# Two sets of tiles that swap parts between the projections and the FFN, the FFN's norm issued behind the projections, and LoRA's second stages among r, k and v

## The chip, the cores and the metric

The kernel runs on one core of one Trainium2 chip. The metric is the time of the whole program on the device in microseconds (us); lower is better. Six streams of instructions run side by side on the core: TensorE (PE, with its weight loads shown as PEld), VectorE (DVE), ScalarE (ACT), GpSimd (POOL), SyncE (SP), which only issues DMAs here, and the DMA engines.

## The reference, cut to what matters

Two layers over 1024 tokens of width 1024, one batch. Each layer is a mixer and an FFN, each behind an RMSNorm that is scaled and shifted by a condition `c`:

```python
for l in range(DEPTH):                                   # DEPTH = 2
    sh1, sc1, gt1, sh2, sc2, gt2 = jnp.split(cond @ ada_w[l] + ada_b[l], 6)
    h = _rmsnorm(x, norm1_g[l]) * (1 + sc1) + sh1
    rw_r, rw_k, rw_v, gl_q, ..., rt_g = jnp.split(h @ w_in[l], splits)   # 24 tiles of 128 columns
    y_a = _rwkv7_mixer(h, rw_r, rw_k, rw_v, ...)   # r, k, v mixed with the token before; w, a, g (and
                                                   # v's residual in layer 1) through LoRA: (f(xw @ w1)) @ w2
    y_b = _gla_mixer(h, ...); y_c = _retention_mixer(...)
    x = x + gt1 * (concat(y_a, y_b, y_c) @ w_out[l])
    h = _rmsnorm(x, norm2_g[l]) * (1 + sc2) + sh2
    x = x + gt2 * ((silu(h @ w_gate[l]) * (h @ w_up[l])) @ w_down[l])    # 2816 wide: 22 tiles
return _rmsnorm(x, norm_f_g)
```

## The kernel before, in words

Activations lie with features on the 128 partitions and 512 tokens (one half, `hf` 0 or 1) along a row. Every large product is done by `dense` (L198): for each of eight (or, in the FFN's last product, three or four) tiles of the contraction it issues three matmuls of 128x128 weights by 512 columns: weight's high part by activation's high part (L207), high by low (L208), low by high (L209). All three add into one PSUM bank of the pool `psd`, which has two. The weight's high part `wh` is a cast by ACT (L186), its low part `wl` a subtraction on POOL (L187); both have three buffers, so the cast for a later tile waits until an earlier product has read its `wh`.

An activation that feeds `dense` is a pair of such parts. In the kernel before, the normed `h` is 8 pairs of 514 columns in the pool `hp`, of which `dense` reads 512 from the third on; the one column before them is the last token of the first half, so that a read shifted by one column is the token shift. The gated products of the FFN and the mixers' output `y` are pairs `gh`, `gl` of 512 columns in the pool `ffn`, read from the first column on.

The order of the work is written out by hand. Main line, (l, hf) for layer and half: `project(0,0)`, `project(0,1)`, then for each half `w_out` (mixers' output through `w_out`, residual), a norm, `ffn`; between the halves' FFNs stands the next layer's `project`. So: `ffn(0,0)`, `w_out(0,1)`, `project(1,0)`, `ffn(0,1)`, `w_out(1,0)`, `project(1,1)`, `ffn(1,0)` with `w_out(1,1)` ahead of its last product, `ffn(1,1)`. The mixers run behind this line as generators in `streams`: after each three matmuls `dense` calls `pump(0.65)`, which lets a stream issue steps worth 0.65 times its rate. `heads` is GLA and retention, `mixers` the RWKV recurrence (a triangular solve of 31 steps on DVE, L914 and L916, per unit of 128 tokens). `drain` runs what is left of the streams at once. A scheduler in the framework then settles the order on each engine.

`project` issues the heads' 13 products (`heads_tiles`), starts the stream of heads (`early`), does LoRA's first stages (`lora_ab`, or `lora_first` in the first call), and then `rkv(p)` for four tiles of 128 columns: three products, each evacuated by ACT (L534), then DVE (L535), and in the first half by a one-column copy on ACT (L538). `lora2(p)` makes LoRA's second stages of tile p: w and a (two matmuls each), in layer 1 u (one), and o (one in f32), L555. w, a and u are evacuated by a tanh on ACT (L404), after which DVE (L405) works in SBUF; o is evacuated by a copy on DVE (L560). In `project(0,0)` `lora2(p)` follows `rkv(p)`. In the other three all four stand after all of `rkv` (`LQ = 3`).

The two `layer_start` calls, around `project(1,0)` and `project(1,1)`, also make the normed `h` for the FFN that follows. Its square sums run as a stream from the start, but its eight steps (`norm`) are passed to `project` as `side`, of which `lora2` takes one after each of its groups: `hp` has room for one `h` alone, and the projections read it to the end. Then `drain` issues the rest of `heads`, and `mixers` starts with the FFN.

Of the kernel before, what the change touches and what calls it, by code (L numbers as in the profile page):

```python
# [10 lines left out]
F32 = mybir.dt.float32  # L11
# [24 lines left out]
LQ = 3  # L36
# [31 lines left out]
XPB = 11  # L68
AHEAD = 60
# [25 lines left out]
def trunk_kernel(ctx, tc, xT, cT, ada_w, pv, wfm, wo, wg, wu, wd, l1w, l2a, l2g, l2c,  # L95
# [163 lines left out]
    def rstd_of(x, idle=None):  # L259
# [29 lines left out]

    def norm_h(x, l, hf, which, h, pool=hp, r=None, mods=None, E=V, idle=None):  # L290
# [36 lines left out]
    def hact(h, shift=0):  # L327
        return lambda k, part: h[k][part][:, 2 - shift:514 - shift]
# [25 lines left out]
    def project(l, hf, h, pool, ip, early=None, first=None, side=None):  # L354
# [173 lines left out]
        def rkv(p):  # L528

            for j in range(3):  # L530
# [11 lines left out]
                more()  # L542

        def lora2(p):
            pcol = slice(p * 128, (p + 1) * 128)
            a = slice(512 + p * 128, 512 + (p + 1) * 128)
            for name, pairs, b_ in (("w", ((l2s[:, pcol], lw), (l2l[0:64, pcol], lw[0:64])), "w0"),
                                    ("a", ((l2s[:, a], la), (l2l[64:128, pcol], la[64:128])), "a0"),
                                    ("u", ((l2v[:, pcol], lv[0:96]),) if l else None, "v0"),
                                    ("o", ((l2gs[:, pcol], lg),), None)):  # L550
                if pairs is None:
                    continue
                ps = bank()
                for i, (w_, a_) in enumerate(pairs):
                    T.matmul(ps, w_, a_, start=i == 0, stop=i == len(pairs) - 1)  # L555
                t = ev()
                if b_:
                    sigmoid(t, ps, l, b_, p)
                else:
                    V.tensor_copy(t, ps)  # L560
                keep(ip, name, t, p)
                step(side)
            if p == 3:
                ip["units"] = True

        if first:
# [496 lines left out]
    def pair_tiles(pool):  # L1063
        return [pool.tile([128, 512], F32R, tag=t, name=t, bufs=8) for t in ("gh", "gl")]

    def y_load(l, hf, y, pool):
        for k in KO:
# [3 lines left out]
            split(t, y[k][0], y[k][1])  # L1071
# [17 lines left out]
    def ffn(l, hf, x, h, before_last=None, side=None):  # L1089
# [6 lines left out]
        def gate_up(f, gt):  # L1096
# [7 lines left out]
            gt.append(pair_tiles(gp))  # L1104
            split(sg, *gt[-1])
# [267 lines left out]
```

## Time and profile before

| | |
|---|---|
| time, median of 3 runs (lowest to highest) | 3398.83 us (3397.83 to 3406.38) |
| time of the profiled execution | 3401.25 us |
| its span | 3399.5 us |
| TensorE clock granted, mean share of full | 0.92 |
| busy: PE / DVE / ACT / POOL | 3049.9 / 1994.5 / 1113.9 / 1234.7 us |
| three matmuls on `h` (L207 to L209) | 2208 of each, 423, 411 and 410 ns |
| three matmuls on `gh`, `gl` | 960 of each, 419, 401 and 400 ns |

Busy time of PE overlaps itself: a matmul is counted from its start to its modelled end, and the next one starts before that. So the spacing of starts, not the mean duration, tells the rate. The clock is either full (1.00) or half (0.50); a stretch's figure is the mean.

### The profile page before, as it was taken

The page shows a single profiled execution, that of the slowest core. Times are in us where ns is not written, and L with a number is a line of the kernel's source. Part 1 is how long each engine was busy: PE and PEld are TensorE (multiplying, and loading weights), DVE is VectorE, ACT ScalarE, POOL GpSimd, SP SyncE. Part 2 cuts the span into 40 slices and gives each one's busy share as a digit, 9 for nine tenths or more (in the row PEclk, how much of TensorE's full clock was granted, in tenths as well). Part 3 has the DMA queues.
Part 4 walks back from the last instruction along what each step waited for, and adds up shares of the span by engine and source line. Part 5 has one row for each costly group of instructions (what it writes and reads, how often), then busy time and mean ns, then how long its engine had stood idle before and what let it go on. Part 6 is the DMA issues. An engine that isn't in the chain of part 4 may idle for free. (4 is left out here: it accounts for less than half of the span.)

```text
span 3399.5 us, 47488 instructions
## 1 busy us (share of the span) xinstructions
PE 3049.9 (90%) x18162; PEld 2326.1 (68%) x18162; DVE 1994.5 (59%) x3747; ACT 1113.9 (33%) x1703; POOL 1234.7 (36%) x825
## 2 busy tenths in 40 slices
PE   6897888799888888999988999899997989999998
PEld 4664666476676676776766777677576767778886
DVE  6565777576776655536766663624666666452223
ACT  4324323243233223524322322542432322342222
POOL 6313333123334334532333434533232433444443
PEclk8988889799989898999988999999897989999999
DMA  6744535434544224434433322543533323332332
GB/s 230 239 157 142 169 110 156 153 103 128 147 129 113 88 84 133 156 90 146 129 98 86 87 70 87 161 130 112 155 83 88 105 80 94 120 109 87 105 92 82
DMA packets 266835, 411.01 MB, mean 121 GB/s; under 512 B 71152, under 2 KB 149424, under 8 KB 266608
## 3 DMA queue, kind: packets, MB, share of 16 engines
q1 hardware_dynamic: 211312, 393.28, 37.2%
q10 hardware_dynamic: 55296, 14.70, 2.1%
q8 instruction: 143, 2.34, 0.3%
q14 instruction: 84, 0.69, 0.1%
HBM read 343.92 MB, written 63.96 MB: 120 GB/s over the span
## 5 line engine op out<-in xcount | busy, mean ns | idle before, releaser
L187 POOL TENSOR_TENSOR wl<-wr,wh 128x1024 fp32r<-128x1024 f32 (+2 forms) x508 | 1028.6, 2027 | 1744.2 <-ACT wh L186 1653.2
L207 PE MATMUL psd<-h,wh 128*128 128x512 f32 (+1 forms) x2208 | 933.2, 423 | 112.7 <-DVE sg L1100 65.7
L208 PE MATMUL psd<-h,wh 128*128 128x512 f32 (+1 forms) x2208 | 908.1, 411 | 12.1 <-DVE h L195 12.0
L209 PE MATMUL psd<-h,wl 128*128 128x512 f32 (+1 forms) x2208 | 905.1, 410 | 0.0
L186 ACT CAST wh<-wr 128x1024 fp32r<-128x1024 f32 (+2 forms) x507 | 440.8, 871 | 1142.0 <-PE psd L208 582.2
L207 PEld LDWEIGHTS psd<-h,wh 128*128 128x128 f32 (+1 forms) x2208 | 432.1, 196 | 249.9 <-DVE sg L1100 74.3
L208 PEld LDWEIGHTS psd<-h,wh 128*128 128x128 f32 (+1 forms) x2208 | 434.7, 197 | 117.2 <-DVE h L195 15.8
L209 PEld LDWEIGHTS psd<-h,wl 128*128 128x128 f32 (+1 forms) x2208 | 433.7, 196 | 103.2 <-issue 2.4
L207 PE MATMUL psd<-gh,wh 128*128 128x512 f32 x960 | 401.0, 419 | 25.9 <-DVE x L1114 14.0
L208 PE MATMUL psd<-gl,wh 128*128 128x512 f32 x960 | 385.0, 401 | 6.1 <-DVE gl L195 6.1
L209 PE MATMUL psd<-gh,wl 128*128 128x512 f32 x960 | 384.0, 400 | 0.0
L207 PEld LDWEIGHTS psd<-gh,wh 128*128 128x128 f32 x960 | 184.7, 193 | 78.6 <-issue 24.1
L1114 DVE SCALAR_TENSOR_TENSOR x<-psd,mod,x 128x512 f32<-128x512 f32 x192 | 143.2, 748 | 130.0 <-PE psd L209 128.4
L208 PEld LDWEIGHTS psd<-gl,wh 128*128 128x128 f32 x960 | 185.6, 193 | 47.0 <-DVE gl L195 9.3
L209 PEld LDWEIGHTS psd<-gh,wl 128*128 128x128 f32 x960 | 185.4, 193 | 40.6 <-POOL wl L187 0.3
L914 DVE TENSOR_TENSOR tm<-X,nl 128x60 f32<-128x60 f32 (+24 forms) x496 | 189.0, 381 | 14.6 <-DMA nl<-nd 0.2
L242 DVE SCALAR_TENSOR_TENSOR aw<-aw,cb 128x1024 f32<-128x1024 f32 x96 | 128.4, 1341 | 100.0 <-DMA aw<-in_ada_w 75.8
L916 DVE TENSOR_TENSOR X<-X,tm 128x60 f32<-128x60 f32 (+24 forms) x496 | 165.1, 333 | 15.3
L1100 DVE SCALAR_TENSOR_TENSOR sg<-sg,psd 128x512 f32<-128x512 f32 x88 | 60.1, 683 | 194.1 <-ACT sg L1099 193.9
L1103 DVE SCALAR_TENSOR_TENSOR sg<-sg,psd 128x512 f32<-128x512 f32 x88 | 60.1, 683 | 141.0 <-PE psd L209 140.8
L195 DVE TENSOR_TENSOR gl<-sg,gh 128x512 fp32r<-128x512 f32 x88 | 96.3, 1094 | 37.0 <-ACT gh L194 36.9
L277 DVE TENSOR_TENSOR acc<-acc,sq 128x512 f32<-128x512 f32 x63 | 96.3, 1528 | 30.9 <-ACT sq L270 29.4
(459 smaller groups left out, 3526.6 us busy)
## 6 DMA issues: line engine op xcount, KB each, us to landing
aw<-in_ada_w SPq DMA_DIRECT2D x96, 512.0 KB, 3.9
wr<-in_wfm SPq DMA_DIRECT2D x96, 512.0 KB, 3.7
wr<-in_wg SPq DMA_DIRECT2D x88, 512.0 KB, 3.6
wr<-in_wu SPq DMA_DIRECT2D x88, 512.0 KB, 3.6
wr<-in_wd SPq DMA_DIRECT2D x128, 256.0 KB, 2.7
wr<-in_wo SPq DMA_DIRECT2D x32, 512.0 KB, 3.6
wr<-in_wd SPq DMA_DIRECT2D x64, 192.0 KB, 2.4
x<-in_xT SPq DMA_DIRECT2D x32, 256.0 KB, 4.5
```

The source lines that it names most:

```text
L186: (E.copy if E is A else E.tensor_copy)(wh[:, :n], wr[:, :n])
L187: WS.tensor_tensor(out=wl[:, :n], in0=wr[:, :n], in1=f32(wh[:, :n]), op=ALU.subtract)
L195: E.tensor_tensor(out=lo, in0=src, in1=f32(hi), op=ALU.subtract)
L207: T.matmul(ps[:M], sh, act(k, 0), start=(k == order[0]), stop=False)
L208: T.matmul(ps[:M], sh, act(k, 1), start=False, stop=False)
L209: mark[:] = [T.matmul(ps[:M], sl, act(k, 0), start=False, stop=(k == order[-1])).ins]
L242: V.scalar_tensor_tensor(out=w, in0=w, scalar=0.5, in1=cb, op0=ALU.mult, op1=ALU.mult, accum_out=mod[l][:, rnd, k:k + 1])
L277: V.tensor_tensor(out=acc, in0=acc, in1=sq, op=ALU.add)
L914: V.tensor_tensor(out=tm[:, :nr, :n], in0=X[:, :nr, s:s + 1].to_broadcast([128, nr, n]), in1=nl[:, s, s + 1:32].unsqueeze(1).to_broadcast( ...
L916: V.tensor_tensor(out=X[:, :nr, s + 1:32], in0=X[:, :nr, s + 1:32], in1=tm[:, :nr, :n], op=ALU.add)
L1100: V.scalar_tensor_tensor(out=sg, in0=sg, scalar=1.0, in1=pg, op0=ALU.add, op1=ALU.mult)
L1114: V.scalar_tensor_tensor(out=x[m], in0=ps, scalar=mod[l][:, 5, m:m + 1], in1=x[m], op0=ALU.mult, op1=ALU.add)
```

## The change

- `h`, gated products and `y` use one kind of tile, `pair_tiles`: a row of 528 columns (`HP = 16` and 512), of which `dense` reads from column 16 on.
- There are two sets of 16 such tiles, `sa` in `hp` and `sb` in `ffn`. The set that holds a projection's `h` takes the gated products of the FFN behind it; the other holds that FFN's `h`. Then they swap.
- So the FFN's norm no longer waits for the projections' last read. In `layer_start` it becomes a stream of its own at rate 0.8, started with the projections; what is left of it at their end is issued there.
- `lora2` makes one name of one tile. `rkv` spreads these among its 12 products: one after each (12 in layer 0), or one, one, two (16 in layer 1).
- In `layer_start` the streams are no longer drained: `later` runs `heads`, and goes on to `mixers` once the projection is over.
- The squares at the very start have four buffers instead of five.

```diff
+HP = 16
@@ rstd_of
-                sq = idle.tile([128, 512], F32, tag="sq", name="sq", bufs=5)
+                sq = idle.tile([128, 512], F32, tag="sq", name="sq", bufs=4)
+    def pair_tiles(pool):
+        return [pool.tile([128, HP + 512], F32R, tag="h", name="h", bufs=16) for _ in range(2)]
@@ norm_h
-            h.append([pool.tile([128, 514], F32R, tag="h", name="h", bufs=16) for _ in range(2)])
+            h.append(pair_tiles(pool))
-            hi, lo = (h[k][j][:, 2:514] for j in range(2))
+            hi, lo = (h[k][j][:, HP:] for j in range(2))
     def hact(h, shift=0):
-        return lambda k, part: h[k][part][:, 2 - shift:514 - shift]
+        return lambda k, part: h[k][part][:, HP - shift:HP + 512 - shift]
@@ project
-        def rkv(p):
-            for j in range(3):
+        def rkv():
+            todo2 = [(p, n) for p in range(4) for n in ("waoh" if not l else "wauo") if n != "h"]
+            n2 = len(todo2)
+            for t3 in range(12):
+                p, j = divmod(t3, 3)
                 i = 4 * j + p
                 ps = dense(get_w(wfm[l, i]), act)
...
                 more()
+                while n2 - len(todo2) < (t3 + 1) * n2 // 12:
+                    lora2(*todo2.pop(0))
-            for p in range(4):
-                rkv(p)
-                if p > LQ:
-                    lora2(p - 1 - LQ)
-            for p in range(3 - LQ, 4):
-                lora2(p)
-        finish(side)
+            rkv()
@@
-    def pair_tiles(pool):
-        return [pool.tile([128, 512], F32R, tag=t, name=t, bufs=8) for t in ("gh", "gl")]
@@ w_out, ffn
-            ps = dense(get_w(wo[l, m]), lambda k, part: y[k][part], order=KO)
+            ps = dense(get_w(wo[l, m]), hact(y), order=KO)
-            gt.append(pair_tiles(gp))
-            split(sg, *gt[-1])
+            gt.append(pair_tiles(gpool))
+            split(sg, *(u[:, HP:] for u in gt[-1]))
@@
-    def first(ip):
-        yield from heads(0, 0, ip)
+    def later(l, hf, ip, B):
+        yield from heads(l, hf, ip)
         while "units" not in ip:
             yield 1.0
-        yield from mixers(0, 0, ip, 2)
+        yield from mixers(l, hf, ip, B)
-    def layer_start(l, hf, h, x):
-        hn, r, ip = [], [], {}
-        def rms():
-            yield 4.0
-            r.append((yield from rstd_of(x)))
+    def layer_start(l, hf, h, x, hpool):
+        hn, ip = [], {}
         def norm():
-            yield from norm_h(x, l if hf else l - 1, 1 - hf, 1, hn, r=r[0])
-        behind(rms(), RATEH)
+            yield 4.0
+            yield from norm_h(x, l if hf else l - 1, 1 - hf, 1, hn, hpool)
+        st = behind(norm(), RATEH)
         with pool("inp") as inp:
-            project(l, hf, h, inp, ip, early=lambda: behind(heads(l, hf, ip), RATEH), side=norm())
-            drain()
+            project(l, hf, h, inp, ip, early=lambda: behind(later(l, hf, ip, 1), RATE2))
+            while st in streams:
+                advance(st)
+        ip["units"] = True
         return ip, hn
@@ main line
+    sa, sb = hp, gp
-            ip, h = layer_start(l + 1, 0, hn, xb)
-            behind(mixers(l + 1, 0, ip), RATE2)
-            ffn(l, 1, xb, h, side=y_load(l + 1, 0, y, gp))
+            ip, h = layer_start(l + 1, 0, hn, xb, sb)
+            ffn(l, 1, xb, h, sa, side=y_load(l + 1, 0, y, sa))
-            xa = w_out(l + 1, 0, y, xp, norm_h(xb, l + 1, 1, 0, hn))
-            ip, h = layer_start(l + 1, 1, hn, xa)
-            behind(mixers(l + 1, 1, ip), RATE2)
+            xa = w_out(l + 1, 0, y, xp, norm_h(xb, l + 1, 1, 0, hn, sb))
+            ip, h = layer_start(l + 1, 1, hn, xa, sa)
```

Line numbers in the new kernel differ: `dense` is L208 to L210, a second stage L566, its tanh L409, the evacuation of r, k, v L542 and L546, the cast of weights L187, the norm L315 and L195.

What moves is seen in the instructions' order. First PE at the end of `project(1,0)`: `h` and `wh` are a product of `dense`, `lw`, `la`, `lv`, `lg` the inputs of the second stages w, a, u and o, `gatt` and `Sa` work of `heads`; in brackets stands the engine whose semaphore a row waits for. Before:

```order
L697 MATMUL yu<-gvt,gatt 64x64 x7
L699 MATMUL yu<-Sa,gqd 64x64 x8
L555 MATMUL psd<-lw,l2s 128x512 [waits Activation_49]
L555 MATMUL psd<-lw,l2l 128x512
L697 MATMUL pm<-gvt,gatt 64x64 [waits PE_49]
L697 MATMUL pm<-gvt,gatt 64x64 x7
L699 MATMUL pm<-Sa,gqd 64x64 x8
L555 MATMUL psd<-la,l2s 128x512 [waits Activation_49]
L555 MATMUL psd<-la,l2l 128x512
L555 MATMUL psd<-lv,l2v 128x512 [waits Activation_49]
```

and now, within r, k and v, first at a w, then at a u with its o:

```order
L210 MATMUL psd<-h,wl 128x512
L566 MATMUL psd<-lw,l2s 128x512 [waits DVE_49]
L566 MATMUL psd<-lw,l2l 128x512
L208 MATMUL psd<-h,wh 128x512 [waits Activation_49]
L209 MATMUL psd<-h,wh 128x512
```

```order
L210 MATMUL psd<-h,wl 128x512
L566 MATMUL psd<-lv,l2v 128x512 [waits Activation_49]
L566 MATMUL psd<-lg,l2gs 128x512 [waits Activation_49]
L208 MATMUL psd<-h,wh 128x512 [waits Activation_49]
L209 MATMUL psd<-h,wh 128x512
```

The block of second stages is gone from the end; each stands between two products, and the product behind it waits for ACT. (In the built program that product has the PSUM bank that the w just ahead of it wrote, and the o has the bank of its u; with o alone, in layer 0, the product behind has o's bank and waits for DVE.)

Second ACT in the same place: `wh<-wr` is the cast of weights, `ev<-psd,mu` the evacuation of r, k or v, `ev<-psd,pvh` the tanh of a second stage, `h<-nt` and `nt<-nt` the FFN's norm. Before:

```order
L186 CAST wh<-wr 128x1024
L534 ACTIVATE ev<-psd,mu_11044 128x512
L701 COPY gqe<-yu 128x4x64
L310 ACTIVATE nt<-nt,mod_84,gs 128x512
L614 ACTIVATE gt<-gqe 128x512
L538 ACTIVATE rkvl<-psd,pv_85 128x1
L404 ACTIVATE ev<-psd,pvh_86 128x512
L194 CAST h<-nt 128x512
L404 ACTIVATE ev<-psd,pvh_86 128x512
L310 ACTIVATE nt<-nt,mod_84,gs 128x512
```

and now, in r, k, v of `project(1,0)`:

```order
L187 CAST wh<-wr 128x1024
L542 ACTIVATE ev<-psd,mu_11044 128x512
L409 ACTIVATE ev<-psd,pvh_86 128x512
L546 ACTIVATE rkvl<-psd,pv_85 128x1
L187 CAST wh<-wr 128x1024
```

and, in its heads' products (L448 evacuates one of these), the norm:

```order
L315 ACTIVATE nt<-nt,mod_84,gs 128x512 x2
L195 CAST h<-nt 128x512 x2
L187 CAST wh<-wr 128x1024
L315 ACTIVATE nt<-nt,mod_84,gs 128x512 x2
L195 CAST h<-nt 128x512
L448 ACTIVATE ev<-psd 128x512
```

The tanh now stands behind the cast and the evacuation at each product, and the norm some 20 products earlier.

Third PE at the end of `project(0,1)`, where unit 3 of the first half's `mixers` ends (L929 to L988 and L962 to L979 are its steps, L1012 the transposes of its last norm). Before:

```order
L929 MATMUL px<-xt,GB 32x32 x16
L555 MATMUL psd<-lg,l2gs 128x512
L938 MATMUL yB<-GB,w_4621 32x32 x16
L555 MATMUL psd<-lw,l2s 128x512
L555 MATMUL psd<-lw,l2l 128x512
L555 MATMUL psd<-la,l2s 128x512
L979 MATMUL pm<-zs,GB 64x64
```

and now:

```order
L988 MATMUL pm<-SV,BK 64x64 x7
L962 MATMUL yA<-SV,GB 64x64 x4
L208 MATMUL psd<-h,wh 128x512
L209 MATMUL psd<-h,wh 128x512
L210 MATMUL psd<-h,wl 128x512
```

```order
L210 MATMUL psd<-h,wl 128x512
L566 MATMUL psd<-lg,l2gs 128x512
L1012 MATMUL pm<-cs_t,Y 128x128 x4
```

Before, the unit's steps stood among the block of second stages, behind the last product; now they stand among the products, and only the last norm is behind them.

More of the change, by code (lines that the diff above doesn't have):

```diff
@@ L35 @@
 YP = 0.0
-LQ = 3
 POSTY = 2.0
@@ L141, in behind @@
         streams.append([gen, rate, 0.0])
+        return streams[-1]
     def advance(st):
@@ L314, in norm_h @@
                     if hf == 0:
-                        G.memset(f32(h[k][j][:, 0:2]), 0.0)
-                        G.tensor_copy(hlast[l][:, k, j:j + 1], f32(h[k][j][:, 513:514]))
+                        G.memset(f32(h[k][j][:, HP - 2:HP]), 0.0)
+                        G.tensor_copy(hlast[l][:, k, j:j + 1], f32(h[k][j][:, HP + 511:HP + 512]))
                     else:
-                        G.tensor_copy(h[k][j][:, 1:2], hlast[l][:, k, j:j + 1])
+                        G.tensor_copy(h[k][j][:, HP - 1:HP], hlast[l][:, k, j:j + 1])
             yield 1.0
@@ L352, in trunk_kernel, with project @@
     carry = {}
-    def project(l, hf, h, pool, ip, early=None, first=None, side=None):
+    def project(l, hf, h, pool, ip, early=None, first=None):
         act = hact(h)
@@ L542, in rkv, with lora2 @@
                 more()
-        def lora2(p):
+                while n2 - len(todo2) < (t3 + 1) * n2 // 12:
+                    lora2(*todo2.pop(0))
+        def lora2(p, name):
             pcol = slice(p * 128, (p + 1) * 128)
[L546 to L564, printed above, removed]
+            if name == "w":
+                pairs, b_ = ((l2s[:, pcol], lw), (l2l[0:64, pcol], lw[0:64])), "w0"
+            elif name == "a":
+                pairs, b_ = ((l2s[:, 512 + p * 128:512 + (p + 1) * 128], la), (l2l[64:128, pcol], la[64:128])), "a0"
+            elif name == "u":
+                pairs, b_ = ((l2v[:, pcol], lv[0:96]),), "v0"
+            else:
+                pairs, b_ = ((l2gs[:, pcol], lg),), None
+            ps = bank()
+            for i, (w_, a_) in enumerate(pairs):
+                mark[:] = [T.matmul(ps, w_, a_, start=i == 0, stop=i == len(pairs) - 1).ins]
+            t = ev()
+            if b_:
+                sigmoid(t, ps, l, b_, p)
+            else:
+                V.tensor_copy(t, ps)
+            keep(ip, name, t, p)
         if first:
@@ L577, in project @@
             lora_ab()
-            for p in range(4):
-                rkv(p)
-                if p > LQ:
-                    lora2(p - 1 - LQ)
-            for p in range(3 - LQ, 4):
-                lora2(p)
-        finish(side)
+            rkv()
     R2 = [slice(0, 64), slice(64, 128)]
@@ L1070, in y_load @@
             y[k] = pair_tiles(pool)
-            split(t, y[k][0], y[k][1])
+            split(t, *(u[:, HP:] for u in y[k]))
             yield
@@ L1204, in trunk_kernel @@
         with pool("inp") as inp:
-            project(0, 0, h, inp, ip, early=lambda: behind(first(ip), RATE0), first=start)
+            project(0, 0, h, inp, ip, early=lambda: behind(later(0, 0, ip, 2), RATE0), first=start)
+            ip["units"] = True
         h = norm_now([x_tile(0, k, 1, x0, 8) for k in range(KT)], 0, 1, 0)
@@ L1212, in trunk_kernel @@
     behind(both(0, 1, ip1), RATE1)
+    sa, sb = hp, gp
     y = {}
-    for _ in y_load(0, 0, y, gp):
+    for _ in y_load(0, 0, y, sb):
         pump(YP)
@@ L1221, in trunk_kernel @@
         if on:
-            ffn(l, 0, xa, h, side=y_load(l, 1, y, gp))
+            ffn(l, 0, xa, h, sb, side=y_load(l, 1, y, sb))
             hn = []
-            xb = w_out(l, 1, y, xp, norm_h(xa, l + 1, 0, 0, hn))
-            ip, h = layer_start(l + 1, 0, hn, xb)
-            behind(mixers(l + 1, 0, ip), RATE2)
+            xb = w_out(l, 1, y, xp, norm_h(xa, l + 1, 0, 0, hn, sa))
+            ip, h = layer_start(l + 1, 0, hn, xb, sb)
             y = {}
-            ffn(l, 1, xb, h, side=y_load(l + 1, 0, y, gp))
+            ffn(l, 1, xb, h, sa, side=y_load(l + 1, 0, y, sa))
             hn = []
-            xa = w_out(l + 1, 0, y, xp, norm_h(xb, l + 1, 1, 0, hn))
-            ip, h = layer_start(l + 1, 1, hn, xa)
-            behind(mixers(l + 1, 1, ip), RATE2)
+            xa = w_out(l + 1, 0, y, xp, norm_h(xb, l + 1, 1, 0, hn, sb))
+            ip, h = layer_start(l + 1, 1, hn, xa, sa)
         else:
```

10 lines of the change are left out of this document (5 added, 5 removed).

## The prediction

> **What bounds the kernel now.** I read the page first: engines, clock, the chain.
>
> ```profile
> span 3399.5 us, 47488 instructions
> PE 3049.9 (90%) x18162; PEld 2326.1 (68%) x18162; DVE 1994.5 (59%) x3747; ACT 1113.9 (33%) x1703; POOL 1234.7 (36%) x825
> PE 25%; DVE 7%; ACT 1%; DMA 1%; issue 1%; ACTq 0%; SPq 0%; DVEq 0%
> ```
>
> PE bounds it, but not everywhere: of the 36% of the span that the chain covers (it is followed back only to about 2190 us), PE has 25, so 0.7; DVE has 7. Which stretches are PE's own is told by the table of windows (length, then busy time of PE, PEld, DVE, ACT, POOL with instructions, then the granted clock).
>
> ```profile
> 163.00:296.00 133.00, 117.44 (x1108) 85.57 (x1106) 76.30 (x180) 37.17 (x65) 30.70 (x23) 0.88 0.48 152
> 515.00:620.00 105.00, 91.04 (x555) 67.97 (x553) 78.51 (x179) 31.20 (x47) 36.13 (x31) 0.90 0.47 143
> 620.00:668.00 48.00, 29.00 (x220) 15.65 (x219) 26.87 (x84) 9.33 (x18) 3.39 (x4) 0.64 0.45 153
> 1390.00:1500.00 110.00, 108.89 (x664) 83.61 (x664) 35.10 (x48) 44.60 (x60) 41.46 (x18) 1.00 0.36 115
> 1500.00:1594.00 94.00, 92.67 (x903) 69.69 (x899) 48.12 (x103) 31.47 (x54) 27.86 (x15) 1.00 0.41 127
> 1594.00:1622.00 28.00, 24.71 (x93) 11.08 (x90) 22.92 (x62) 16.14 (x28) 2.71 (x1) 0.60 0.61 209
> 2409.00:2437.00 28.00, 24.02 (x101) 10.95 (x95) 23.15 (x61) 16.16 (x27) 3.27 (x2) 0.62 0.59 201
> 3045.00:3365.00 320.00, 320.00 (x1387) 260.74 (x1386) 86.49 (x98) 84.80 (x118) 140.19 (x79) 1.00 0.31 91
> ```
>
> Rows 1 to 3 are the r, k, v of `project(0,0)`, those of `project(0,1)`, and the end of the first half's mixers. Rows 4 and 5 are `project(1,0)`: PE is busy 201.6 of 204 us at full clock, with DVE at 83 and ACT at 76. Rows 6 and 7 are the second stages at the ends of `project(1,0)` and `project(1,1)`: PE looks busy, but at a clock of 0.60 and 0.62. The last row is the last FFN, PE without a gap.
>
> **Start of the rows that PE streams.** The change moves every `h` from column 2 of a 514-wide row to column 16 of a 528-wide one, and this touches the commonest instruction of all. The timeline of PE in the last FFN, first and last of 25 starts on `h`, then of 52 on `gh`, `gl` (start, duration):
>
> ```profile
> 3099.78 0.39 PE L207 MATMUL psd<-h,wh 128*128 128x512 f32 x1
> ...
> 3105.37 0.39 PE L207 MATMUL psd<-h,wh 128*128 128x512 f32 x1
> ...
> 3149.85 0.39 PE L207 MATMUL psd<-gh,wh 128*128 128x512 f32 x1
> ...
> 3161.41 0.39 PE L207 MATMUL psd<-gh,wh 128*128 128x512 f32 x1
> ```
>
> On `h` a start follows the last after 5.59/24 = 232.9 ns, on the gated tiles after 11.56/51 = 226.7: same size, same weights' shape, full clock, no waits. What differs is where the row starts: column 2 against column 0. Column 16 is 64 bytes in, so I take 226.7 for it, as the nearer row; the bounds are no gain and 6.2 ns each. The groups give the counts:
>
> ```profile
> L207 PE MATMUL psd<-h,wh 128*128 128x512 f32 (+1 forms) x2208 | 933.2, 423 | 112.7 <-DVE sg L1100 65.7
> L207 PE MATMUL psd<-gh,wh 128*128 128x512 f32 x960 | 401.0, 419 | 25.9 <-DVE x L1114 14.0
> ```
>
> Three times 2208 are 6624 matmuls, at most 41 us. Where PE never rests the gain is whole: 2 x 600 in `project(1,0)` and `project(1,1)`, 1056 in the last FFN, 2256 x 6.2 = 14.0. The three FFNs with mixers behind them have 3168, 19.6 us; of these I take 0.7 (PE's share of the chain) times a clock of 0.9, 12.4, since waits for the streams grow where PE gets faster. The first two projections have 1200, 7.4 us, and are half the mixers': 3. Together **-29**.
>
> The Trainium skill (TensorE: Matmul & The Clock Gate, "Wait — 56ns, not 53.3ns?") gives the spacing of full-clock matmuls as columns over 2.4 GHz plus about 2.5 ns, 215.7 ns for 512, with no word on where the row starts; by that this term would be nothing. The trace has two spacings, neither of them that.
>
> **Second stages: what a wait costs.** `project(0,0)` already has them between products. PE, ACT, DVE there (in brackets the idle time and who ended it):
>
> ```profile
> 267.62 0.39 PE L209 MATMUL psd<-h,wl 128*128 128x512 f32 x1
> 267.86 0.40 PE L555 MATMUL psd<-lw,l2s 128*128 128x512 f32 x1
> 268.18 0.50 PE L555 MATMUL psd<-lw,l2l 64*128 64x512 f32 x1
> 270.13 0.49 PE L555 MATMUL psd<-la,l2s 128*128 128x512 f32 x1 [1.45 <-ACT ev L404]
> 271.16 1.23 PE L555 MATMUL psd<-lg,l2gs 128*128 128x512 f32 x2
> 271.87 0.94 PE L207 MATMUL psd<-h,wh 128*128 128x512 f32 x1
> ...
> 267.87 1.05 ACT L186 CAST wh<-wr 128x1024 fp32r<-128x1024 f32 x1 [4.91 <-DMA wr<-in_l1w]
> 268.82 0.68 ACT L534 ACTIVATE ev<-psd,mu 128x512 f32<-128x512 f32 x1
> 269.40 0.68 ACT L404 ACTIVATE ev<-psd,pvh 128x512 f32<-128x512 f32 x1
> ...
> L535 DVE SCALAR_TENSOR_TENSOR ev<-psd,pv,ev 128x511 f32<-128x511 f32 x48 | 35.7, 745 | 39.1 <-ACT ev L534 39.0
> L560 DVE COPY ev<-psd 128x512 f32<-128x512 f32 x16 | 11.0, 687 | 11.4 <-DMA ip_v<-ev 6.2 <-PE psd L555 5.2
> ```
>
> When a product ends, ACT first casts the next weights (its last read frees `wh`), then evacuates the product, then does the tanh: 267.86 to 270.08. The matmul that wants the tanh's bank starts at 270.13, with PE idle 1.45. After the change the order shows just this row of ACT at every tile, and the next product in the tanh's bank. So a w or an a costs 1.45 us of waiting (0.77 where heads' matmuls, some 0.68 us, stand ahead of it); an o that wants its u's bank 270.13 - 267.86 - 0.43 = 1.84 (1.15); an o alone in layer 0 waits for DVE behind L534's end at 269.50: 269.50 + 0.75 + 0.69 - 267.86 - 0.71 = 2.3.
>
> `project(1,0)` and `project(1,1)`, each: the order has 5 w or a without and 3 with heads' work ahead, 2 and 2 u with o: 5 x 1.45 + 3 x 0.77 + 2 x 1.84 + 2 x 1.15 = 15.5 us of new waits. What goes is the block:
>
> ```profile
> 2408.41 0.39 PE L209 MATMUL psd<-h,wl 128*128 128x512 f32 x1
> ...
> 2409.96 0.49 PE L555 MATMUL psd<-lw,l2s 128*128 128x512 f32 x1
> ...
> 2436.54 1.42 PE L207 MATMUL psd<-h,wh 128*128 128x512 f32 x1
> ```
>
> It takes 26.6 us, in which the stages' own matmuls at full clock are 4 x (0.85 + 0.85 + 0.43 + 0.71) = 11.4 and heads' about 2; 13 are lost, and 1 more until the clock is back. With 2.5 for the clock (below) that is 15.5 + 2.5 - 14 = +4 each, **+8**. The norm's 8 x 4 instructions on DVE and ACT go into the heads' products at no cost: rows 4 and 5 leave both engines over half idle, and a product's evacuation has the next product's 5.6 us. If that cover went, ACT would be late with `wh`. The rest of heads and the mixers slide some 6 us into the FFN, inside the last down products' slack.
>
> `project(0,0)`: three waits of its four blocks, 0.8 to 1.45 us, become twelve: by the order 4 x 1.45 + 3 x 0.77 + 4 x 2.3 - 0.7 = 16.6, against 4.5 and a slow clock after the third block (3.4 us at half, 1.7 lost). Half of the rise covers waits that DVE's heads make there anyway: **+6**.
>
> `project(0,1)`: the block stood in front of the mixers' tail.
>
> ```profile
> 627.26 0.79 PE L555 MATMUL psd<-la,l2s 128*128 128x512 f32 x1 [7.16 <-DVE ev L535]
> 664.85 1.08 PE L1012 MATMUL pm<-cs_t,Y 128*128 128x128 f32 x4 [7.00 <-DVE Y L625]
> 668.80 0.79 PE L208 MATMUL psd<-gl,wh 128*128 128x512 f32 x1 [2.44 <-DVE gl L195]
> ```
>
> From 620 to 668 PE runs at a clock of 0.64, and `w_out` starts only when unit 3's last norm is through. By the new order unit 3's steps stand among the products and only L1012 is left behind. Up to 24 us could go (half of 48); against it stand twelve waits of 1.45 to 2.3, some 20 us, in a stretch where DVE is busy 78.5 of 105. I take **-9**, bounds -24 and +12.
>
> **The clock.** A window of 3.41 us that PE fills too little is followed by half clock:
>
> ```profile
> 1094.66:1098.08 3.42, 1.95 (x9) 1.65 (x10) 3.21 (x11) 0.00 (x0) 0.00 (x0) 1.00 0.46 135
> 1098.08:1101.49 3.41, 3.41 (x16) 2.78 (x15) 2.90 (x8) 1.58 (x2) 1.34 (x1) 1.00 0.81 328
> 268.64:272.05 3.41, 1.85 (x6) 0.84 (x5) 2.42 (x4) 2.39 (x5) 2.42 (x2) 1.00 0.38 143
> 272.05:275.46 3.41, 3.41 (x9) 2.62 (x9) 0.23 (x1) 0.40 (x1) 0.61 (x2) 0.50 0.90 202
> ```
>
> 1.95 busy (0.57) was let pass, 1.85 (0.54) was not. A wait of 1.45 leaves 1.96, just above; 1.84 or 2.3 leaves less, if it falls in one window, which half of some ten do: five closings of one or two windows, 2.5 us each, about a half of it in the two later projections (2.5 each, counted above), the rest within +6 and -9.
>
> The same page ("What's actually happening") has the clock go down after an idle window; by it none of these waits would, and the sum would be some 10 us lower. The row at 268.64 speaks against it.
>
> Sum: -29 + 8 + 6 - 9 = -24 on 3401.25 us of the profiled execution, 3377. That execution is 2.4 above the median of 3398.83, so on the medians: **3375 us**, 0.7% faster. Its own range: with the start's gain between 24 and 35 and the tail between +3 and -21 it goes from 3375 - 6 - 12 = 3357 to 3375 + 5 + 12 = 3392.
>
> **Rivals.** *The start of the row is not what spaces the matmuls.* Then the 29 is gone and the rest, -24 + 29 = +5, stands: 3404. For it: I infer the cause from two kinds of tile. Against: 6.2 ns over 25 and 52 starts in the same stretch. The Trainium skill's formula, quoted above from that page, is this rival. Chance 0.15.
>
> *The waits close the clock* (slower). Place: the product behind each second stage, 48 of them in the four projections. At 0.57 busy a wait of 1.45 lies 0.03 above what closed it at 268.64. A closing of two windows costs 6.8/2 = 3.4 us. Beyond seven closings more than the five the gain of 24 is eaten, from ten more on it is slower by over 0.3%; if a third of the 48 close it, eleven more, and DVE's lag in `project(0,1)` is paid in full (+12 instead of -9), it is 3375 + 37 + 21 = 3433. Chance 0.17.
>
> *The chains are freed more than counted*: the tail of `project(0,1)` goes whole (-24 instead of -9) and the closings in `project(1,0)` and `project(1,1)` stay out (-5): 3355. For it: the 0.64. Against: DVE's 78.5 of 105. Chance 0.13.
>
> That the change does not do what it says, the order excludes: norm and stages have moved.
>
> **How the numbers follow.** 0.3%, 10 us, is about what a measurement of this kernel can tell from no change. Forecast 0.55 (0.51 faster, 0.04 same); first rival 0.15 (0.02, 0.09, 0.04 slower); second 0.17 (0.02, 0.05, 0.10); third 0.13, faster. That makes 0.68 faster, 0.18 same, 0.14 slower. The range takes in the third rival below and the first above, with some of the second: 3345 to 3412.
>
> **What the profile after would show.** Starts on `h` 226.7 ns apart, and mean durations of `h` as of the gated tiles; else the first term is wrong. No stretch at a clock of 0.6 ahead of the FFNs, where rows 6 and 7 stand. Twelve idle times of 0.8 to 2.3 us on PE in each projection, ended by ACT's tanh or DVE's copy; were they over 3 us or followed by a clock of 0.5 at most tiles, the second rival holds. `w_out` nearer to the last product of `project(0,1)`; were the distance still 50 us, the -9 falls.

## The result and the profile after

| | before | after |
|---|---|---|
| median of 20 runs (lowest to highest) | 3398.05 us (3382.08 to 3406.38) | 3419.11 us (3396.94 to 3434.13) |
| ratio (time over that of the kernel before in the same series) | | 1.0059, 95% interval 1.0042 to 1.0076 |
| a second series: median | 3399.05 us | 3425.14 us, 1.0075 (1.0051 to 1.0099) |
| the profiled execution: span, clock | 3399.5 us, 0.920 | 3396.8 us, 0.931 |

The change makes the kernel 20 us slower; 24 us less were forecast. The profiled execution of the changed kernel lies at the low end of its runs, 20 us under the median, so below the profiles tell where time goes, and the medians how much of it there is. The page after:

```profile
span 3396.8 us, 47494 instructions
PE 3026.1 (89%) x18162; PEld 2306.9 (68%) x18162; DVE 2019.6 (59%) x3747; ACT 1116.3 (33%) x1705; POOL 1233.5 (36%) x825
PE 24%; DVE 7%; DMA 2%; ACT 2%; issue 1%; ACTq 0%; POOL 0%; SPq 0%; DVEq 0%; POOLq 0%
```

PE is busy 24 us less and idle 21 us more than before (370.7 us against 349.5, counting what no matmul covers). Two things on it changed. First the starts in the last FFN: the timeline of PE, first and last of 192 starts on `h`, then of 96 on the gated tiles (which are also called `h` now).

```profile
3092.61 0.40 PE L208 MATMUL psd<-h,wh 128*128 128x512 f32 x1
...
3136.76 0.39 PE L210 MATMUL psd<-h,wl 128*128 128x512 f32 x1
3136.99 0.39 PE L208 MATMUL psd<-h,wh 128*128 128x512 f32 x1
...
3158.95 0.39 PE L210 MATMUL psd<-h,wl 128*128 128x512 f32 x1
```

44.15/191 = 231.1 ns on `h`, where 232.9 were before and 226.7 forecast; and 21.96/95 = 231.2 on the gated tiles, where 226.7 were before. The one got 1.8 ns better, the other 4.5 worse, and the last FFN as a whole, from its first product to the end, takes 384.0 us against 383.5.

Second r, k, v and second stages of `project(1,0)` and `project(1,1)`, into the FFN's first product. Windows before (length, busy time of PE, PEld, DVE, ACT, POOL, clock):

```profile
1500.20:1623.00 122.80, 118.18 (x984) 81.37 (x983) 71.72 (x164) 47.61 (x81) 30.57 (x16) 0.91 0.46 147
2312.10:2438.60 126.50, 121.60 (x1027) 83.97 (x1024) 74.70 (x167) 45.82 (x71) 35.79 (x27) 0.91 0.47 144
```

and after:

```profile
1506.90:1634.50 127.60, 110.11 (x944) 77.65 (x943) 61.48 (x121) 37.69 (x64) 29.45 (x16) 0.96 0.39 126
2315.50:2447.80 132.30, 115.59 (x986) 81.72 (x985) 64.29 (x124) 35.56 (x54) 36.34 (x27) 0.95 0.39 122
```

The clock is better, as forecast (0.96 and 0.95 for 0.91), but PE, which rested 4.6 and 4.9 us before, now rests 17.5 and 16.7, and both stretches are longer, by 4.8 and 5.8 us. The view of PE's waits names who is waited for in the first of them (us in all, times, longest):

```profile
PE psd L208 <- ACT ev L409: 9.7, 8, 1.5
PE psd L566 <- ACT ev L409: 5.1, 4, 1.9
PE psd L208 <- ACT rkvl L546: 2.7, 1, 2.7
```

Twelve waits for the tanh, as the order said: eight behind a w or an a (three of about 0.8 us, five of 1.46), four of an o for its u's bank (three of 0.97 to 1.17, one of 1.89). And one that was not foreseen: behind an o the next product got the bank of the last r, k or v, whose last reader is ACT's one-column copy (in `project(1,1)`, which has no such copy, DVE, 2.3 us).

### The profile page after: what moved, and what is told of

Same layout as the page of the kernel before. It is cut to its first block, busy times and chain, and to the rows that moved or that the text cites. A ratio compares the mean times of both kernels' runs of the same rounds, so it can differ in the third digit from the quotient of the medians.

```text
span 3396.8 us, 47494 instructions
## 1 busy us (share of the span) xinstructions
PE 3026.1 (89%) x18162; PEld 2306.9 (68%) x18162; DVE 2019.6 (59%) x3747; ACT 1116.3 (33%) x1705; POOL 1233.5 (36%) x825
## 5 line engine op out<-in xcount | busy, mean ns | idle before, releaser
L208 PE MATMUL psd<-h,wh 128*128 128x512 f32 (+2 forms) x3168 | 1339.7, 424 | 178.5 <-DVE sg L1097 37.5
L209 PE MATMUL psd<-h,wh 128*128 128x512 f32 (+2 forms) x3168 | 1290.2, 407 | 15.3 <-DVE h L196 15.3
L210 PE MATMUL psd<-h,wl 128*128 128x512 f32 (+2 forms) x3168 | 1292.0, 408 | 0.0
L208 PEld LDWEIGHTS psd<-h,wh 128*128 128x128 f32 (+2 forms) x3168 | 615.1, 194 | 384.9 <-issue 57.6
L187 ACT CAST wh<-wr 128x1024 fp32r<-128x1024 f32 (+2 forms) x507 | 441.1, 871 | 1189.2 <-PE psd L209 683.2
L209 PEld LDWEIGHTS psd<-h,wh 128*128 128x128 f32 (+2 forms) x3168 | 618.6, 195 | 161.5 <-DVE h L196 22.7
L210 PEld LDWEIGHTS psd<-h,wl 128*128 128x128 f32 (+2 forms) x3168 | 616.3, 195 | 144.9 <-issue 1.9
L916 DVE TENSOR_TENSOR X<-X,tm 128x60 f32<-128x60 f32 (+24 forms) x496 | 170.3, 343 | 14.8
L914 DVE TENSOR_TENSOR tm<-X,nl 128x60 f32<-128x60 f32 (+24 forms) x496 | 165.6, 334 | 16.2 <-DMA nl<-nd 1.7
L196 DVE TENSOR_TENSOR h<-sg,h 128x512 fp32r<-128x512 f32 x88 | 98.5, 1119 | 26.2 <-ACT h L195 25.8
L195 ACT CAST h<-sg 128x512 fp32r<-128x512 f32 x88 | 54.5, 619 | 152.6 <-DVE sg L1100 148.6
L315 ACT ACTIVATE nt<-nt,mod,gs 128x512 f32<-128x512 f32 x64 | 51.4, 813 | 65.7 <-DVE nt L314 34.1
L486 PE MATMUL psd<-h,wh 128*128 128x512 f32 x128 | 57.0, 448 | 14.1 <-ACT h L195 12.6
L314 DVE TENSOR_TENSOR nt<-x,acc 128x512 f32<-128x512 f32 x58 | 47.5, 833 | 36.4 <-ACT acc L284 35.7
L271 ACT ACTIVATE sq<-x 128x512 f32<-128x512 f32 x71 | 44.1, 629 | 60.1 <-DMA x<-in_xT 16.5
## 6 DMA issues: line engine op xcount, KB each, us to landing
wr<-in_wd SPq DMA_DIRECT2D x128, 256.0 KB, 2.7
x<-in_xT SPq DMA_DIRECT2D x32, 256.0 KB, 4.3
```

Source lines behind the costliest of these rows:

```text
L187: (E.copy if E is A else E.tensor_copy)(wh[:, :n], wr[:, :n])
L196: E.tensor_tensor(out=lo, in0=src, in1=f32(hi), op=ALU.subtract)
L208: T.matmul(ps[:M], sh, act(k, 0), start=(k == order[0]), stop=False)
L209: T.matmul(ps[:M], sh, act(k, 1), start=False, stop=False)
L210: mark[:] = [T.matmul(ps[:M], sl, act(k, 0), start=False, stop=(k == order[-1])).ins]
L914: V.tensor_tensor(out=tm[:, :nr, :n], in0=X[:, :nr, s:s + 1].to_broadcast([128, nr, n]), in1=nl[:, s, s + 1:32].unsqueeze(1).to_broadcast( ...
```

## The experiments

All are kernels of one core, timed beside runs of the kernel before; what is compared directly is mostly of one series, and across series, which ran on different chips, the ratios are used. Behind a time stand its ratio and, in brackets, the 95% interval of the ratio; 0.001 is 3.4 us, and a difference between two of these ratios is known to some 9 us either way, to 12 where a kernel has only six runs. The changed kernel was taken once more:

> The changed kernel once more, for a second profile and a time in the same series as the others. Its first profile lies at the low end of its runs (3398.6 us against a median of 3419). Theory W (the second stages' waits close the clock in some executions more than in others): about 3419, and where this profile is longer than the first one, the r, k, v stretches of the four projections are, by 10 to 20 us together, at half clock. Theory S (the streams behind the FFNs run later, since heads are no longer drained): the FFNs are longer instead, and the r, k, v stretches the same within 5 us.

It took 3425.14 us; its profile is 13.7 us longer than the first. Between the same products, r, k, v of the four projections differ by +0.2, -0.3, -2.0 and +0.4 us; `ffn(0,0)` is 2.8 longer and `ffn(0,1)` 11.2, with 24 us more at half clock. So one execution differs from the next by how the FFNs with mixers fall, which is where theory S looked for it, and W as written there (more closings of the clock in some executions than in others) is out. That the second stages' waits cost the same in every execution is still possible, so the next runs have to tell the two apart.

### Second stages back in blocks, and one project at a time

```diff
-                while n2 - len(todo2) < (t3 + 1) * n2 // 12:
+                while todo2 and (t3 == 11 or first and j == 2 and todo2[0][0] == p):
                     lora2(*todo2.pop(0))
```

> The changed kernel with the second stages where they stood before: behind each four of r, k, v in project(0,0), in one block at the end of the other three. Theory W: the waits go, 3395 to 3403, 15 to 20 us less than the changed kernel. Theory S: 3412 to 3420, no different from the changed kernel. Theory R (the rows of 528 columns decide): also no different, about 3415.

Measured 3382.86 us, 0.9955 (0.9933 to 0.9977): the second stages among the products cost some 40 us, twice what W expected, and what is left of the change is a gain of 15. The same two windows of this kernel:

```profile
1496.20:1615.70 119.50, 114.59 (x944) 78.34 (x943) 56.83 (x130) 38.29 (x64) 29.73 (x16) 0.91 0.45 144
2298.20:2422.00 123.80, 118.91 (x988) 81.26 (x985) 59.76 (x133) 36.51 (x54) 34.77 (x27) 0.91 0.44 139
```

8.1 and 8.5 us shorter than in the changed kernel, at the lower clock. Three more kernels keep the second stages among the products in one place only (`or l == 1 and n2 - len(todo2) < ...` added to the condition above, and so on):

> The changed kernel with the second stages among the products in project(1,0) and project(1,1) alone; in the other two they stand as before. The prediction's term (+8 for both): 3391, against 3383 with all in blocks. By the two profiles of the changed kernel, where these two projections took 6 to 10 us each more than in a block: 3397 to 3401; above 3405 if the lateness also spoils the FFNs behind.

> The same for project(0,1) alone. The prediction's term (the tail behind it goes, -9): 3374. If the tail is DVE's own chain, which ends when it ends (the profiles: r, k, v 7 us shorter, w_out behind it 8 to 11 us longer): 3383 to 3388.

> The same for project(0,0) alone. The prediction's term: +6, 3389. By the profiles (r, k, v 7.5 us longer, the norm behind it 4 shorter, the next heads 3 longer): 3388 to 3391.

Measured 3402.96 us (1.0029, 1.0012 to 1.0046), 3387.85 (0.9975, 0.9959 to 0.9992) and 3381.17 (0.9965, 0.9947 to 0.9982). Against the ratio of `block` that is +25, +7 and +3 us, together the 35 to 41 that lie between `block` and the two series of the changed kernel. Only the +25 is clear of the 9 us; the +7 excludes the forecast -9, and neither it nor the +3 is distinguishable from nothing. The two projections of layer 1 are the bulk. In `project(0,1)` the forecast gain is there and is given back one stage later; windows of r, k, v with the tail, from the second product on, then of `w_out(0,0)` with the norm, in `spread01`:

```profile
517.70:663.10 145.40, 110.63 (x750) 80.73 (x749) 102.00 (x261) 37.70 (x60) 37.61 (x32) 0.86 0.43 134
663.10:754.50 91.40, 83.59 (x829) 60.16 (x827) 61.91 (x97) 34.65 (x50) 19.63 (x9) 0.89 0.42 135
```

and in `block`:

```profile
514.70:670.80 156.10, 120.03 (x774) 84.13 (x773) 106.33 (x264) 39.88 (x63) 39.65 (x34) 0.81 0.46 144
670.80:754.70 83.90, 80.38 (x828) 58.47 (x826) 57.48 (x93) 33.85 (x50) 19.48 (x9) 0.93 0.38 121
```

10.7 us less, then 7.5 more at a clock of 0.89 instead of 0.93. The first product, ahead of these windows, took 4.2 us longer, so from its start to that of the FFN it is 256.0 us against 255.1: nothing is left of the gain.

### The cast behind the tanh

```diff
+            lasts = []
...
-                ps = dense(get_w(wfm[l, i]), act)
+                ps = dense(get_w(wfm[l, i], last=lasts[t3 - WHB] if t3 >= WHB else None), act)
...
+                lasts.append(la_)
@@ split_w
-            (E.copy if E is A else E.tensor_copy)(wh[:, :n], wr[:, :n])
+            with tc.issue_after(last) if last else nullcontext():
+                (E.copy if E is A else E.tensor_copy)(wh[:, :n], wr[:, :n])
```

`la_` is ACT's last instruction behind a product, its evacuation or the tanh.

> The changed kernel; among r, k and v the cast of the weights three products ahead is put behind the evacuation and the tanh on ACT instead of ahead of them, nothing else. Theory W (the product behind a second stage waits for the tanh, and the tanh for the cast): the waits behind w and a fall from 1.45 and 0.78 us to about 0.4 and 0.1, those of o behind its u by the same 1.05; some 8 to 10 us less in each of the four projections, fewer closings of the clock behind them, in all 3380 to 3390 against 3420. Rival (the second stages cost by being there, or by the heads' order, not by the wait): within 8 us of the changed kernel, 3412 to 3425.

Measured 3383.19 us, 0.9959 (0.9941 to 0.9977), with every second stage where the change put it: 34 to 39 us are back, as much as the blocks gave, and S is out as the main cause. In the profiles, r, k, v of the four projections are 34 us shorter together (9.9, 4.9, 9.0 and 10.5). In layer 1 the new order has nothing else to mend: in the two windows of `block` no product of r, k or v waits for ACT. The timeline of PE and ACT at one a of `project(1,0)`, in the changed kernel:

```profile
1584.22 0.39 PE L210 MATMUL psd<-h,wl 128*128 128x512 f32 x1
1584.45 0.39 PE L566 MATMUL psd<-la,l2s 128*128 128x512 f32 x1
1584.46 1.04 ACT L187 CAST wh<-wr 128x1024 fp32r<-128x1024 f32 x1 [6.10 <-PE psd L209]
1585.41 0.68 ACT L542 ACTIVATE ev<-psd,mu 128x512 f32<-128x512 f32 x1
1585.99 0.68 ACT L409 ACTIVATE ev<-psd,pvh 128x512 f32<-128x512 f32 x1
1586.72 0.50 PE L208 MATMUL psd<-h,wh 128*128 128x512 f32 x1 [1.46 <-ACT ev L409]
```

and in `late`:

```profile
1573.13 0.39 PE L211 MATMUL psd<-h,wl 128*128 128x512 f32 x1
1573.37 0.40 PE L570 MATMUL psd<-la,l2s 128*128 128x512 f32 x1
1573.57 0.69 ACT L545 ACTIVATE ev<-psd,mu 128x512 f32<-128x512 f32 x1 [5.68 <-PE psd L211]
1574.28 0.69 ACT L410 ACTIVATE ev<-psd,pvh 128x512 f32<-128x512 f32 x1
1575.02 0.50 PE L209 MATMUL psd<-h,wh 128*128 128x512 f32 x1 [0.83 <-ACT ev L410]
```

The wait falls from 1.46 to 0.83, not to the 0.4 expected, in part since the evacuation starts 0.2 later behind L211 than the cast did behind the last read of `wh`. But over the whole stretch the change is larger than the waits:

```profile
1499.40:1618.20 118.80, 106.74 (x947) 75.21 (x944) 55.83 (x121) 37.27 (x64) 29.34 (x16) 1.00 0.42 136
2308.80:2430.60 121.80, 110.11 (x985) 77.97 (x984) 58.88 (x124) 35.92 (x54) 35.14 (x27) 1.00 0.40 133
```

8.8 and 10.5 us less than in the changed kernel, of which 5.4 and 5.0 are idle time of PE and the rest the clock: 0.96 and 0.95 there, 1.00 here. What closed it, in windows of the changed kernel of one period of the clock each:

```profile
1542.46:1545.87 3.41, 1.94 (x9) 1.09 (x8) 1.54 (x2) 2.47 (x4) 2.08 (x1) 1.00 0.01 4
1545.87:1549.29 3.42, 3.42 (x27) 2.38 (x33) 0.57 (x1) 0.59 (x1) 0.29 (x1) 0.50 0.34 120
1583.42:1586.83 3.41, 1.95 (x9) 1.10 (x7) 0.80 (x2) 2.21 (x3) 1.25 (x1) 1.00 0.69 223
1586.83:1590.25 3.42, 3.42 (x17) 2.83 (x18) 1.84 (x4) 0.26 (x1) 1.13 (x1) 1.00 0.94 313
2354.83:2358.24 3.41, 2.00 (x10) 1.15 (x9) 1.65 (x2) 2.21 (x3) 2.14 (x1) 1.00 0.00 0
2358.24:2361.66 3.42, 3.42 (x78) 2.29 (x75) 0.51 (x1) 0.59 (x1) 0.56 (x2) 1.00 0.63 119
2365.07:2368.49 3.42, 2.00 (x30) 1.32 (x31) 2.10 (x2) 1.57 (x3) 2.69 (x2) 1.00 0.02 5
2368.49:2371.90 3.41, 3.41 (x21) 2.25 (x17) 0.00 (x0) 0.37 (x1) 0.00 (x0) 0.50 0.70 240
```

A wait of 1.41 to 1.47 inside one period leaves 1.94 to 2.00 busy, and the clock may then close or not: of seven periods that hold such a wait whole, three were followed by half clock (1.94, 2.00 and 2.00 busy) and four were not (1.95, 1.95, 2.00 and 1.99). So it is no sharp edge of busy time. In `late`, where most of these waits are 0.78 to 0.83, the clock stays full in both stretches.

### Heads drained or not

```diff
-            project(l, hf, h, inp, ip, early=lambda: behind(later(l, hf, ip, 1), RATE2))
-            while st in streams:
-                advance(st)
-        ip["units"] = True
+            project(l, hf, h, inp, ip, early=lambda: behind(heads(l, hf, ip), RATEH))
+            drain()
+        ip["units"] = True
+        behind(mixers(l, hf, ip), RATE2)
```

> The changed kernel with heads drained at the end of project(1,0) and project(1,1), and the mixers started with the FFN as before. Theory S: 3400 or below. Theory W and R: within 5 us of the changed kernel, 3413 to 3423.

> The second stages in a block as in the kernel 'block', and heads drained at the end of project(1,0) and project(1,1) as in 'nolater': of the change, the rows, the two sets and the FFN's norm as a stream are left. If the block alone gives the gain of 'block' (3383), this is 3380 to 3390; if not draining the heads is what gains there, once the second stages do not disturb it, this falls back to 3395 to 3400.

With the second stages among the products it gave 3406.96 us (1.0030, 1.0009 to 1.0051), 10 to 15 us less than the changed kernel, between what S and what W expected; in a block 3382.89 (0.9942, 0.9919 to 0.9965), no difference. `blocknl` isolates the rows, the sets and the norm's new place: these alone gain 20 us by the ratio, 14 by the medians. In its profile the gain is in the FFNs with mixers: `ffn(0,1)` 510.3 us against 522.1 before, `ffn(1,0)` up to `w_out(1,1)` 461.4 against 478.6. The first is no more than executions differ by (510.6 and 521.8 in the two of the changed kernel); the second is there in every profile with the norm's new place (456 to 467, against 475.6 in `h16`). In `ffn(1,0)` it is one stretch, from the mixers' first solve to the second; before:

```profile
2492.00:2600.00 108.00, 90.42 (x505) 68.07 (x505) 67.65 (x147) 26.81 (x45) 32.63 (x24) 0.79 0.31 82
```

and in `blocknl`:

```profile
2495.00:2583.00 88.00, 78.19 (x518) 61.03 (x516) 67.71 (x143) 26.58 (x46) 32.40 (x23) 0.94 0.35 99
```

The work is the same (DVE 67.7 us in both); PE is at 0.94 instead of 0.79. Which of the three brings this, the norm's move, the two sets or their rows, was not taken apart.

### Rows

> The kernel before with h alone in rows of 528 columns read from column 16; gated products and y stay in rows of 512, and the order of the work stays (the squares at the start have four buffers, for room). Theory R (what spaces the starts is how far apart the rows lie that follow one another, not the column at which a row starts): 231.4 ns on h as in the changed kernel, 227 on the gated tiles as before, so at most 1.2 x 6624 = 8 us off, about 5 on the time: 3393. The prediction's theory (column 16 instead of 2 gives 226.7): 227 on h, 3370.

```diff
-            h.append([pool.tile([128, 514], F32R, tag="h", name="h", bufs=16) for _ in range(2)])
+            h.append([pool.tile([128, 528], F32R, tag="h", name="h", bufs=16) for _ in range(2)])
-        return lambda k, part: h[k][part][:, 2 - shift:514 - shift]
+        return lambda k, part: h[k][part][:, 16 - shift:528 - shift]
```

Measured 3394.77 us, 0.9980 (0.9959 to 1.0001): 4 us by the medians, 7 by the ratio, where the prediction's theory wanted 29. Its last FFN, 192 starts on `h` and 96 on `gh`, `gl`:

```profile
3092.80 0.40 PE L207 MATMUL psd<-h,wh 128*128 128x512 f32 x1
...
3136.96 0.39 PE L209 MATMUL psd<-h,wl 128*128 128x512 f32 x1
3137.19 0.39 PE L207 MATMUL psd<-gh,wh 128*128 128x512 f32 x1
...
3158.74 0.39 PE L209 MATMUL psd<-gh,wl 128*128 128x512 f32 x1
```

44.16/191 = 231.2 and 21.55/95 = 226.8. In its profile the last FFN is 0.9 us shorter (1.7 ns on 1056 matmuls are 1.8), `ffn(0,1)` 1.9 longer and `ffn(1,0)` 3.0 shorter; for the two with mixers that is less than executions differ by. Two more kernels, run for their profiles alone, tell the column from the distance of rows:

> For the spacing of starts alone, not for time: the kernel before with h in rows of 576 columns read from column 64, gated products and y in rows of 528 read from column 0, and two buffers instead of three for the low part of weights (for room). If the column read from decides, h stays at 231 and the gated tiles at 227. If the distance of rows decides, the gated tiles go to 230 or 231, and h, at 2304 bytes (nine times 256), to 227 if a multiple of 256 is enough.

> For the spacing of starts alone: h in rows of 544 columns (2176 bytes, 17 times 128) read from column 32, gated products and y in rows of 576 read from column 0, two buffers for the low part. If the distance decides and a multiple of 128 is enough, both are at 227; if it takes 256, the gated tiles are at 227 and h between 227 and 231; if it takes more (512 to 2048), both are near 231. If the column decides, the gated tiles are at 227 and h at 231.

`p1`, the same counts:

```profile
3108.58 0.39 PE L207 MATMUL psd<-h,wh 128*128 128x512 f32 x1
...
3151.90 0.39 PE L209 MATMUL psd<-h,wl 128*128 128x512 f32 x1
3152.12 0.40 PE L207 MATMUL psd<-gh,wh 128*128 128x512 f32 x1
...
3174.08 0.39 PE L209 MATMUL psd<-gh,wl 128*128 128x512 f32 x1
```

`p2`:

```profile
3095.11 0.40 PE L207 MATMUL psd<-h,wh 128*128 128x512 f32 x1
...
3138.83 0.39 PE L209 MATMUL psd<-h,wl 128*128 128x512 f32 x1
3139.06 0.40 PE L207 MATMUL psd<-gh,wh 128*128 128x512 f32 x1
...
3160.63 0.39 PE L209 MATMUL psd<-gh,wl 128*128 128x512 f32 x1
```

| row, columns (read from) | neighbouring rows lie apart by (places modulo 256 bytes in which rows start) | spacing of starts |
|---|---|---|
| 514 (2), `h` before | 2080 bytes = 65 x 32 in the built program (eight) | 232.9 ns |
| 528 (16 or 0), `h16`, after; gated in `p1` | 2112 = 33 x 64 (four) | 231.2, 231.1; 231.2 |
| 544 (32), `h` in `p2` | 2176 = 17 x 128 (two) | 228.9 |
| 576 (64 or 0), `h` in `p1`; gated in `p2` | 2304 = 9 x 256 (one) | 226.8; 227.1 |
| 512 (0), gated before and in `h16` | 2048 = 8 x 256 (one) | 226.7, 226.8 |

The column does not matter: 528 from column 0 is as slow as from column 16, 576 from 64 as fast as from 0. LoRA's first stages in `late576` read the same rows of `h` from column 64 and from column 63: 229.2 and 227.9 ns (92 and 103 starts at full clock with nothing between). What goes with the spacing is the layout as a whole: rows that all start in one place modulo 256 bytes, or in two, four or eight. It is not the distance from one row to the next in the stream, as theory R has it. In `p1` the two parts of a gated tile lie 8 x 2112 = 66 x 256 bytes apart in the built program, and yet the steps from one to the other and back take 232.0 and 229.9 ns in the last FFN. What in the chip makes it so no run shows. The last runs use the layout on top of `late`:

> The kernel 'late' with rows of 576 columns read from column 64 in both sets, so that all rows start a multiple of 256 bytes apart; for room the weights' low part has two buffers, x ten and the squares at the start three. Theory R (the distance of the rows spaces the starts): 227 ns on all, 4.5 ns less on 9504 matmuls, which shows only where PE never rests: about 300 in the heads' products of project(1,0) and of project(1,1), some 1400 in the last FFN and the w_out ahead of it, 400 more in the first stages and w_out: 2400 x 4.5 = 11 us, so 3372 against 3383. If the FFNs with mixers gained too, 3345. If two buffers cost more than the rows give: 3383 or above.

> 'late' with the fewer buffers of 'late576' alone, rows of 528 as before. If the buffers cost nothing: 3383. The difference of 'late576' from this one is then the rows'.

> 'late576' with heads drained at the end of project(1,0) and project(1,1). In a block this made no difference (3383 both); with second stages whose waits are short it should make none either: within 6 us of 'late576'.

> The kernel 'late' with rows of 544 columns read from column 32 in both sets and of 576 read from column 64 for the last FFN's h, three buffers for the weights' low part as in 'late', ten for x. Theory R: 229 ns in the sets and 227 on the last h, 2.3 ns less on about 1300 matmuls and 4.5 on 1056 where PE never rests, some 8 us: 3375 against 3383 of 'late'. If ten buffers for x were what cost 'latectl' its 20 us, 3395 instead; if the rows give nothing, 3383.

`late576` took 3379.88 us (0.9933, 0.9908 to 0.9959), its control `latectl` 3403.90 (1.0000, 0.9976 to 1.0024), `latenl576` 3396.66 (0.9981, 0.9957 to 1.0004). The rows give 24 us there, known to 12, where 11 were expected, and the fewer buffers take 14 (by the ratios) to 21: in the heads' products of `project(1,0)` PE is idle 6.9 us with two buffers for the low part, 3.2 with three. Draining heads lost 17 us here, where no more than 6 were expected, gained 10 to 15 in the changed kernel and did nothing in a block; the cause of that is open.

`mix544` keeps the three buffers for the low part and has ten for x, so the ten are not what cost `latectl` its time: 3374.28 us, 0.9927 (0.9904 to 0.9950), the lowest of all, 23 us under the kernel before in its series and 45 to 50 under the change by the ratios. Its interval overlaps that of `late`; in the profile its last FFN takes 379.4 us against 383.9, where 4.4 ns on 1056 matmuls and 2.3 on 528 are 5.9.

## Why the prediction was wrong

**Start of the rows (-29, measured about 0).** The step that failed is "Column 16 is 64 bytes in, so I take 226.7 for it". `h` and gated tiles differed in two things, the column and the layout of their rows, and I named one without a row that told them apart. `p1` and `p2` show it is the other. So the change won 1.8 ns on 6624 matmuls, 12 us, and lost 4.5 on 2880, 13 us; in the last FFN, where PE never rests, that is +0.5 us. The second step, that FFNs with mixers pass on 0.63 of such a gain, no run settles: `h16` gains 7 us by its ratio of the 11 that 1.7 ns on 6624 make, known to 7 us either way. The first rival was right that column 16 instead of 2 gains nothing; that `h` gets a little faster and the gated tiles slower it did not have, and that the two cancel is luck.

**Second stages in layer 1 (+8, measured +25 by the ratios).** The kind and number of the waits for the tanh were right, twelve, and so was their sum, 14.8 us for 15.5. Summed from start to start in `project(1,0)`, changed kernel against `block`: waits 17.5 us instead of 4.9; the stages' own matmuls 11.9 instead of 19.7, most of which ran at half clock; products slowed by the clock +3 (forecast 2.5). That is +8.1, and +8.5 in `project(1,1)`, where +4 each was written. The terms that failed are the thirteenth wait, 2.7 us, which the sum did not have, and the block's loss, 12.7 rather than 14. The remaining 8 of the 25 are not in these stretches. The stretch from `ffn(1,0)` to `ffn(1,1)` is 4.9 us longer in the profile of `spread1` than in `block`, but 5.7 and 6.7 longer in `spread01` and `spread00`, which have these stages in blocks; so the profiles do not place the 8, and they are less than the 9 to which the 25 is known.

**`project(0,1)` (-9, measured +7).** The gain in r, k, v was there, 10.7 us, by the mechanism named. What I left out is that it can be taken back around them: 4.2 us in the first product and 7.5 in `w_out`, at a clock of 0.89 instead of 0.93. Nor are all twelve waits "1.45 to 2.3": in `spread01` PE waits 16.2 us in two places, 8.5 in one, for DVE's copy of an o (L572), which I had at 2.3.

**`project(0,0)` (+6, measured +3).** The size agrees within what is known, the mechanism does not. I wrote that half of the rise covers waits which are there anyway; in `spread00` r, k, v took 13.5 us longer, the whole of the rise of 12. It came back later: 14.4 less in r, k, v of `project(0,1)`, and from the first product of r, k, v to the first of `ffn(0,0)` 599.9 us against 599.7 in `block`.

**The norm at no cost (0, measured with the sets -15 to -20).** It was costed as work that hides, and is one: PE's stretch in the heads' products of `project(1,0)` grew 1.6 us. That `ffn(1,0)` would get shorter was not in the sum.

**The clock.** "A wait of 1.45 leaves 1.96, just above" was right in the time that is left, 1.94 to 2.00, and wrong in "just above": three of seven such periods closed the clock. In the changed kernel's two projections of layer 1 it closed five times, where five were forecast for all four; the other two are at the waits of 1.89 and 1.83 us for an o's bank. The Trainium skill (TensorE: Matmul & The Clock Gate, "A second HAM failure mode: psum-queue depth-cycling") tells of short idle times between groups of matmuls that make the clock swing. The rows at 1542.46 and 1545.87 agree with it, and `late` shows how little less wait is enough. The second rival, whose place this is, came nearest with 3433 (14 us off, the first 15), and that is luck: it is paid in closings of the clock, and the clock in these stretches was better than before; what was paid is PE waiting.

The sum with the measured terms: 0 + 25 + 7 + 3 - 15 = +20, which is the result. With terms known to 7 to 9 us each, that it comes out to the unit is luck.

## What to carry to other kernels

When short operations are put between long products, look who evacuates them and what stands ahead of that evacuation in its engine's queue: here a cast of 1.04 us that nobody was waiting for, ahead of a tanh that PE was waiting for, cost 34 to 39 us in four projections, and was mended by a rule of order for that cast. Two groups of instructions that differ in speed usually differ in more than one thing; change each alone in a small run before a term is built on one of them. A gain on PE counts where PE never rests, and a gain ahead of a stage can be taken back in it: follow each term to the next point where all engines meet.

## What was not expected of the hardware

Matmuls of 512 fp32r columns at full clock started 226.7 to 227.1 ns apart when the rows that they stream all start in one place modulo 256 bytes, 228.9 with two places, 231.1 to 231.2 with four and 232.9 with eight; the column from which a row was read made no difference in the cases tried. And a period of 3.41 us in which PE is busy 1.94 to 2.00 us may close the clock or not: three of seven did.
